# Moving the activation buffers of a two-layer hybrid decoder from byte 192 (and, for one buffer, byte 0) to byte 64, modulo 256, of the weight buffers

## The chip, the core and the metric

One core of one Trainium2 chip runs the whole program. The metric is the time of one execution in microseconds, the median of several runs. The engines are called PE (TensorE, matmuls), PEld (its weight loads, which overlap the matmuls), DVE (VectorE), ACT (ScalarE), POOL (GpSimd) and SP (the queue that issues the DMAs here).

A matmul reads two operands from the core's on-chip memory (SBUF). The *stationary* operand, always 128 columns here, is loaded first, by a weight load of its own; the *moving* operand, 128, 256 or 512 columns, is then streamed past it. While one matmul streams, the load for the next one already runs.

## The reference

The input is 256 tokens of width 1024 in float32. Two layers follow each other, each with a token mixer and a SwiGLU block, each part behind an RMS norm and with a residual add:

```python
y = rms_norm(h, norm_mix[0]);  h = h + hgrn2_mixer(y, ...)   # 8 heads, projections [q|forget|input|gate]
h = h + swiglu(rms_norm(h, norm_ffn[0]), ffn_w13[0], ffn_w2[0])
y = rms_norm(h, norm_mix[1]);  h = h + moba_mixer(y, ...)    # 8 heads, causal attention with a bias table
h = h + swiglu(rms_norm(h, norm_ffn[1]), ffn_w13[1], ffn_w2[1])
return rms_norm(h, final_norm)

def swiglu(h, w13, w2):                     # hidden width 2816
    g, u = jnp.split(h @ w13, 2, axis=-1)
    return (jax.nn.silu(g) * u) @ w2
```

The gated recurrence (HGRN2) is evaluated in levels, with products of the forget gates; with 256 tokens the attention has one block and is plain causal attention.

## The kernel before

**Weights.** All weight matrices are streamed once, in 206 pieces (`raw`, one DMA each, mostly 128 x 1024). ACT rounds a piece to a high part `whi` (line 412) and DVE subtracts to get the low part `wlo` (line 414). Both go into rings of 6 buffers of 4096 bytes a partition. A 128-column piece of a weight begins at a multiple of 512 bytes in its buffer.

**Activations.** Each activation tile, too, is a high and a low part, of 128 x 256: `xh{k}`, `xl{k}` for the eight slices of a layer's input, in two buffers each that alternate from one use to the next, and `hh{n}`, `hl{n}` for the hidden tiles of the SwiGLU block (n = 0 to 6, hidden tile j uses n = j mod 7). The hidden tiles take over the rings of the recurrence's scaled queries and keys `q1, q2, q4 ... q64` and `k1 ... k64` (`alias`): hh0 and hl0 lie where q1 and k1 lay, again with two buffers that alternate.

**Matmuls.** Every product of a weight and an activation is made of three matmuls (high x high, low x high, high x low), all through line 455. There are two forms. In `mm_w` the weight piece is stationary and the activation moves, 256 columns: the projections by head, the output projections, both gate and up products, and the down product of layer 0. In `mm_x` the activation is stationary and the weight moves, 512 columns: the input and value projections and the down product of layer 1. The products among activations (recurrence scores, attention) are a small rest.

**Order.** A planner in the kernel (`Order`) decides at build time, with costs of its own, in which order each engine's instructions stand. In a SwiGLU block 48 matmuls of a gate and up pair alternate with those of a down product: 24 of 256 columns in layer 0 (to psB), 12 of 512 columns in layer 1 (to psA).

**Layout.** `lay_out` makes the first buffers in a fixed order, one behind the other, so that their places are known: a spacer `lead`, the weight rings (which begin at a multiple of 256 bytes), a spacer `gap`, the activation rings, the query and key rings. Everything else follows behind. q1 and k1 have buffers of 1216 bytes instead of 1024 and spacers of 64 bytes on both sides, which puts the first buffer of each at byte 0 modulo 256 and the second at byte 192.

Of the kernel before, what the change touches and what calls it, by code (L numbers as in the profile page):

```python
# [8 lines left out]
FT = mybir.dt.float32  # L9
# [6 lines left out]
P = 128  # L16
S = 256
# [285 lines left out]
def hybrid_trunk(ctx: ExitStack, tc: tile.TileContext, wts, xT, par, gfin, tab, onehot, masks, out):  # L303
# [4 lines left out]
    sb = ctx.enter_context(tc.tile_pool(name="sb", bufs=1))  # L308
# [3 lines left out]
    rings = {}  # L312

    def ring(tag, shape, bufs, dt=FT):
        if tag not in rings:
            rings[tag] = Ring(lambda: sb.tile(shape, dt, name=tag, tag=tag, bufs=bufs), bufs)
        return rings[tag]
# [4 lines left out]
    def alias(tag, other, shape, dt=FT):  # L322

        o = rings[other]
        wide = [P, S + 48] if other in ("q1", "k1") else shape
        rings[tag] = Ring(lambda: sb.tile(wide, dt, name=tag, tag=other, bufs=o.bufs)[:, :shape[1]], o.bufs)
        rings[tag].past = o.past

    def lay_out():


        sb.tile([P, 96], FT, name="lead")
        for t in ("whi", "wlo"):
            ring(t, [P, SUB], NSUB, FR).make()
        sb.tile([P, 48], FT, name="gap")
        for k in range(KT):
            for part in "hl":
                ring(f"x{part}{k}", [P, S], 2, FR).make()
        for part in "qk":

            sb.tile([P, 16], FT, name=f"gap{part}1")
            rings[f"{part}1"] = Ring(lambda part=part: sb.tile([P, S + 48], FT, name=f"{part}1", tag=f"{part}1",
                                                              bufs=2)[:, :S], 2)
            rings[f"{part}1"].make()
            sb.tile([P, 16], FT, name=f"gap{part}2")
        for m in (2, 4, 8, 16, 32, 64):
            for part in "qk":
                ring(f"{part}{m}", [P, S], 2).make()

# [30 lines left out]
    plan = weight_plan()  # L380
    RAW, NSUB = 6, 6
    lay_out()
    segs, c0 = [], 0
    for n in FIRST + (SUB,) * ((NCOLS - sum(FIRST)) // SUB):
# [529 lines left out]
    for n, m in enumerate((1, 2, 4, 8, 16, 32, 64)):  # L914
        alias(f"hh{n}", f"q{m}", [P, S], FR)
        alias(f"hl{n}", f"k{m}", [P, S], FR)
    alias("lg", "mov", [P, 2, 192])
    alias("pt", "sq", [P, 512])
    x1 = {k: X("x", k) for k in range(KT)}
# [371 lines left out]
```

## Time and profile before

| | |
|---|---|
| median of 3 runs | 629.64 us (629.41 to 631.18) |
| span of the profiled execution, first to last instruction | 629.2 us |
| PE busy | 617.4 us, 98% of the span, 4848 matmuls |
| DVE, ACT busy | 441.0 us (70%), 364.2 us (58%) |
| read from device memory | 109.78 MB, 176 GB/s over the span |
| mean granted PE clock | 0.995 |

The median stands 0.4 us above the profiled span. In the profile a matmul's duration goes from its start to the end of its results, so the durations of neighbours overlap; how fast matmuls follow each other is read from the chain of work that ended last, which gives a start, a length and a count for each stretch: length by count is the distance from one matmul to the next. In a row like `psB<-xh,whi` the names are output, moving operand, stationary operand; in a form with the weight moving the weight stands first. The stages of the execution are: input projection to 28 us, recurrence to 137 us, its output projection to 167 us, SwiGLU of layer 0 to 328 us, value projection and norm to 357 us, attention with its projections to 444 us, output projection to 466 us, SwiGLU of layer 1 to 622 us, final norm.

### The profile page before, as it was taken

The page shows a single profiled execution, that of the slowest core. Times are in us where ns is not written, and L with a number is a line of the kernel's source. Part 1 is how long each engine was busy: PE and PEld are TensorE (multiplying, and loading weights), DVE is VectorE, ACT ScalarE, POOL GpSimd, SP SyncE. Part 2 cuts the span into 40 slices and gives each one's busy share as a digit, 9 for nine tenths or more (in the row PEclk, how much of TensorE's full clock was granted, in tenths as well). Part 3 has the DMA queues.
Part 4 walks back from the last instruction along what each step waited for, and adds up shares of the span by engine and source line. Part 5 has one row for each costly group of instructions (what it writes and reads, how often), then busy time and mean ns, then how long its engine had stood idle before and what let it go on. Part 6 is the DMA issues. An engine that isn't in the chain of part 4 may idle for free.

```text
span 629.2 us, 12441 instructions
## 1 busy us (share of the span) xinstructions
PE 617.4 (98%) x4848; PEld 594.2 (94%) x4848; DVE 441.0 (70%) x800; ACT 364.2 (58%) x715; POOL 39.2 (6%) x74
## 2 busy tenths in 40 slices
PE   7999999999999999999999999999999999999995
PEld 5899999999999999999998899999899999999994
DVE  5898878877786666666659678866686666666653
ACT  6798888875564444444446566564674444444443
POOL 0132112200400000000000000000100000000003
PEclk9999999999999999999999999999999999999998
DMA  8964443534896666666653564445545665555501
GB/s 273 324 217 136 154 128 123 155 115 134 209 282 200 194 199 198 190 189 198 201 189 116 209 223 160 143 154 182 180 160 197 201 199 197 177 188 176 168 1 67
DMA packets 32135, 111.83 MB, mean 178 GB/s; under 512 B 3835, under 2 KB 4508, under 8 KB 32076
## 3 DMA queue, kind: packets, MB, share of 16 engines
q1 hardware_dynamic: 31052, 108.71, 53.4%
q0 software_dynamic: 448, 1.25, 1.0%
q10 hardware_dynamic: 576, 1.08, 0.6%
q8 instruction: 38, 0.62, 0.4%
q14 instruction: 21, 0.17, 0.1%
HBM read 109.78 MB, written 1.25 MB: 176 GB/s over the span
## 4 chain that ended last, share of the span: by engine, by line
PE 78%; issue 16%; DVE 3%; DMA 1%; ACT 1%; POOL 1%; SPq 0%; ACTq 0%; DVEq 0%; POOLq 0%
PE psB L455 44%; PE psA L455 33%; DMA raw<-in_w_dram 1%; DVE wlo L414 1%; POOL ny L591 1%; DVE xl L541 0%; DVE yt L607 0%; ACT whi L412 0%; DVE hT L609 0%; DVE sqacc L559 0%; PE psB L1146 0%; SPq L401 0%; SPq L522 0%; PE psA L596 0%; DVE raw L1177 0%
## 5 line engine op out<-in xcount | busy, mean ns | idle before, releaser
L414 DVE TENSOR_TENSOR wlo<-raw,whi 128x1024 fp32r<-128x1024 f32 (+1 forms) x206 | 247.8, 1213 | 107.8 <-ACT whi L412 107.4
L412 ACT ACTIVATE whi<-raw 128x1024 fp32r<-128x1024 f32 (+1 forms) x205 | 213.0, 1050 | 145.7 <-issue 66.7
L455 PE MATMUL psB<-xh,whi 128*128 128x256 f32 x608 | 172.6, 287 | 0.0
L455 PE MATMUL psB<-xh,wlo 128*128 128x256 f32 x608 | 167.6, 279 | 0.0
L455 PE MATMUL psB<-xl,whi 128*128 128x256 f32 x608 | 163.3, 279 | 0.0
L455 PE MATMUL psA<-xh,whi 128*128 128x256 f32 x544 | 150.3, 280 | 0.0
L455 PE MATMUL psA<-xh,wlo 128*128 128x256 f32 x544 | 148.8, 277 | 0.0
L455 PE MATMUL psA<-xl,whi 128*128 128x256 f32 x544 | 144.0, 277 | 0.0
L455 PEld LDWEIGHTS psB<-xh,wlo 128*128 128x128 f32 x608 | 114.6, 188 | 0.7
L455 PEld LDWEIGHTS psB<-xh,whi 128*128 128x128 f32 x608 | 114.4, 188 | 0.8
L455 PEld LDWEIGHTS psB<-xl,whi 128*128 128x128 f32 x608 | 112.2, 189 | 0.0
L455 PEld LDWEIGHTS psA<-xh,whi 128*128 128x128 f32 x544 | 102.4, 188 | 0.6 <-issue 0.5
L455 PEld LDWEIGHTS psA<-xh,wlo 128*128 128x128 f32 x544 | 102.2, 188 | 0.0
L455 PEld LDWEIGHTS psA<-xl,whi 128*128 128x128 f32 x544 | 99.2, 188 | 0.0
L455 PE MATMUL psB<-hl,whi 128*128 128x256 f32 x176 | 48.7, 277 | 0.0
L455 PE MATMUL psB<-hh,whi 128*128 128x256 f32 x176 | 48.7, 277 | 0.0
L455 PE MATMUL psB<-hh,wlo 128*128 128x256 f32 x176 | 48.7, 276 | 0.0
L957 ACT ACTIVATE u<-sgq 128x256 f32<-128x256 f32 x44 | 18.0, 410 | 38.9 <-DVE sgq L955 38.7
L455 PE MATMUL psA<-wlo,hh 128*128 128x512 f32 x88 | 34.6, 393 | 0.0
L455 PE MATMUL psA<-whi,hl 128*128 128x512 f32 x88 | 34.5, 392 | 0.0
L455 PE MATMUL psA<-whi,hh 128*128 128x512 f32 x88 | 34.5, 392 | 0.0
L455 PEld LDWEIGHTS psB<-hl,whi 128*128 128x128 f32 x176 | 33.1, 188 | 0.0
(178 smaller groups left out, 793.8 us busy)
## 6 DMA issues: line engine op xcount, KB each, us to landing
raw<-in_w_dram SPq DMA_DIRECT2D x202, 512.0 KB, 4.2
raw<-in_w_dram SPq DMA_DIRECT2D x4, 256.0 KB, 3.3
bt<-scr POOLq DMA_DIRECT2D x8, 128.0 KB, 9.1
hT<-in_x_dram SPq DMA_DIRECT2D x4, 128.0 KB, 5.1
hT<-in_x_dram SPq DMA_DIRECT2D x2, 256.0 KB, 8.1
bt<-in_final_dram ACTq DMA_DIRECT2D x1, 512.0 KB, 5.4
out_dram<-raw ACTq DMA_DIRECT2D x2, 256.0 KB, 2.2
out_dram<-raw SPq DMA_DIRECT2D x2, 256.0 KB, 2.0
```

The source lines that it names most:

```text
L412: od.op("A", ca(n), lambda h=h, r=r, o=o, n=n: A.activation(h[:, :n], r[:, o:o + n], AF.Copy), reads=[r], alloc=[h], due=due)
L414: od.op("V", cv(n), lambda h=h, lo=lo, r=r, o=o, n=n: V.tensor_tensor(lo[:, :n], r[:, o:o + n], h[:, :n].bitcast(FT), op=OP.subtract), rea ...
L455: T.matmul(o, a, b, start=start, stop=stop, skip_group_check=True)
L591: od.op("G", 500, lambda: G.tensor_tensor(y.tile, v.tile, mhalf, op=OP.pow), reads=[v], alloc=[y], due=due)
L957: od.op("A", ca(S), lambda: A.activation(sg.tile, gs.tile, AF.Sigmoid), reads=[gs], alloc=[sg], due=due)
```

## The change

Only the places of buffers change. The spacer behind the weights shrinks from 192 to 64 bytes, the extra width and the spacers of q1 and k1 go.

```diff
     def alias(tag, other, shape, dt=FT):
         o = rings[other]
-        wide = [P, S + 48] if other in ("q1", "k1") else shape
-        rings[tag] = Ring(lambda: sb.tile(wide, dt, name=tag, tag=other, bufs=o.bufs)[:, :shape[1]], o.bufs)
+        rings[tag] = Ring(lambda: sb.tile(shape, dt, name=tag, tag=other, bufs=o.bufs), o.bufs)
         rings[tag].past = o.past
 
     def lay_out():
         sb.tile([P, 96], FT, name="lead")
         for t in ("whi", "wlo"):
             ring(t, [P, SUB], NSUB, FR).make()
-        sb.tile([P, 48], FT, name="gap")
+        sb.tile([P, 16], FT, name="gap")
         for k in range(KT):
             for part in "hl":
                 ring(f"x{part}{k}", [P, S], 2, FR).make()
-        for part in "qk":
-
-            sb.tile([P, 16], FT, name=f"gap{part}1")
-            rings[f"{part}1"] = Ring(lambda part=part: sb.tile([P, S + 48], FT, name=f"{part}1", tag=f"{part}1",
-                                                              bufs=2)[:, :S], 2)
-            rings[f"{part}1"].make()
-            sb.tile([P, 16], FT, name=f"gap{part}2")
-        for m in (2, 4, 8, 16, 32, 64):
+        for m in (1, 2, 4, 8, 16, 32, 64):
             for part in "qk":
                 ring(f"{part}{m}", [P, S], 2).make()
```

First byte of the buffers in a partition, modulo 256:

| | before | after |
|---|---|---|
| whi, wlo | 0 | 0 |
| xh, xl; hh1 to hh6, hl1 to hl6 (q2 to q64, k2 to k64) | 192 | 64 |
| hh0, hl0 (q1, k1): first, second buffer | 0, 192 | 64, 64 |
| hT, u, xsf, ff, mov | 32 | 160 |
| raw | 96 | 224 |
| sgq | 160 | 32 |

On every engine the same instructions stand in the same order in both programs, with the same waits; only the numbers at the end of some buffer names differ.

## Prediction

> **What bounds the kernel now.** I read the busy times first, then the chain that ended last, then the busy times by stage.
>
> ```profile
> PE 617.4 (98%) x4848; PEld 594.2 (94%) x4848; DVE 441.0 (70%) x800; ACT 364.2 (58%) x715; POOL 39.2 (6%) x74
> PE 78%; issue 16%; DVE 3%; DMA 1%; ACT 1%; POOL 1%; SPq 0%; ACTq 0%; DVEq 0%; POOLq 0%
> ...
> 167.00:328.00 161.00, 161.00 (x1420) 161.00 (x1419) 104.59 (x147) 76.84 (x104) 0.79 (x2) 1.00 0.67 206
> ...
> 526.00:608.00 82.00, 82.00 (x592) 77.23 (x591) 51.64 (x68) 37.52 (x49) 0.00 (x0) 1.00 0.49 159
> ```
>
> The stage rows give the stretch, its length, then the busy time of PE, PEld, DVE, ACT and POOL, the granted clock and the DMA share. PE never idles in either SwiGLU stage, the clock is full, and DVE and ACT have a third of the time to spare. So the end is set by how closely matmuls follow each other, and a nanosecond on each shows in the sum. The chain shows that this distance isn't one number. Start, length, work, count, first in layer 0, then in layer 1:
>
> ```profile
> 184.14 5.46 PE psA L455 x48
> 189.59 2.72 PE psB L455 x24
> 192.31 5.44 PE psA L455 x48
> ...
> 290.23 5.44 PE psA L455 x48
> 295.67 2.86 PE psB L455 x24
> ...
> 516.01 2.75 PE psA L455 x12
> 518.75 5.47 PE psB L455 x48
> 524.22 2.73 PE psA L455 x12
> 526.96 5.66 PE psB L455 x48
> 532.61 2.77 PE psA L455 x12
> 535.38 5.66 PE psB L455 x48
> ```
>
> Call *relation* the byte of the moving operand minus that of the stationary one, modulo 256. The x48 rows have relation 192 (weights at 0, activations at 192), and so have the x24 rows but the one at 295.67: there the hidden tile is j = 14, whose hh0 and hl0 lie at byte 0, relation 0. (j = 0 has these buffers too; j = 7 and 21 have the second ones, at 192.) From these rows:
>
> - relation 192, 256 columns: 5.44 us / 48 = 113.3 ns, or 5.66 / 48 = 117.9 ns. Two paces, each steady for long.
> - relation 0, 256 columns: 2.86 / 24 = 119.2 ns, against 2.72 / 24 = 113.3.
> - 512 columns, where activation and weight change roles: at byte 192 the relation is 0 - 192 = 64: 2.75 / 12 = 229.2 ns, or 2.77 / 12 = 230.8. The group at 524.22 is tile j = 7 with its buffers at byte 0, relation 0: 2.73 / 12 = 227.5. Twice the shortest distance of 256 columns would be 226.7.
>
> So places do matter, by up to 6 ns a matmul, and the row at 524.22 is followed by a change of pace (5.47 to 5.66) that lasts to 608 us: the pace has a memory, set by what came before, and the place alone doesn't fix it.
>
> How much is lost in all at relation 192? In the groups by line, the mean duration of a matmul is 276 ns in the stretch from 200 to 290 us (113.3 apart) and 281 ns from 527 to 608 us (117.9 apart). Below are one row of each stretch, and then the rows of the whole execution:
>
> ```profile
> L455 PE MATMUL psA<-xh,wlo 128*128 128x256 f32 x176 | 48.6, 276 | 0.0
> ...
> L455 PE MATMUL psB<-xh,wlo 128*128 128x256 f32 x160 | 45.0, 281 | 0.0
> ```
>
> ```profile
> L455 PE MATMUL psB<-xh,whi 128*128 128x256 f32 x608 | 172.6, 287 | 0.0
> L455 PE MATMUL psB<-xh,wlo 128*128 128x256 f32 x608 | 167.6, 279 | 0.0
> L455 PE MATMUL psB<-xl,whi 128*128 128x256 f32 x608 | 163.3, 279 | 0.0
> L455 PE MATMUL psA<-xh,wlo 128*128 128x256 f32 x544 | 148.8, 277 | 0.0
> L455 PE MATMUL psA<-xl,whi 128*128 128x256 f32 x544 | 144.0, 277 | 0.0
> L455 PE MATMUL psB<-hl,whi 128*128 128x256 f32 x176 | 48.7, 277 | 0.0
> L455 PE MATMUL psB<-hh,wlo 128*128 128x256 f32 x176 | 48.7, 276 | 0.0
> ```
>
> Over the floor of 276 ns stand 3 ns on 3 x 608 (I give the first row, which also holds restarts after the recurrence's small matmuls, the value of its two sisters), 1 ns on 3 x 544 and 0.6 ns on 3 x 176: 5.5 + 1.6 + 0.3 = 7.4 us of duration. Five ns of duration are 4.6 ns of distance, so 6.8 us of the span, 1.7 ns for each of 3984 matmuls of 256 columns.
>
> **The change part by part.** It adds and removes no instruction, wait or transfer, and moves none in its queue. What it changes is the relation: 256 columns go from 192 (and 0) to 64, 512 columns from 64 (and 0) to 192. Products among activations keep relation 0.
>
> *256 columns.* No matmul of 256 columns has relation 64 before. Bounds from the nearest rows: 113.3 ns below (nothing lost, a gain of 6.8 us), 119.2 above (5.9 x 3984 = 23.5 us lost in place of 6.8, so 16.7 us worse). Nearest is the only row at relation 64, the 512-column one: 229.2 - 226.7 = 2.5 ns lost per matmul. It has no clean stretch: both paces of the 256-column rows around it leave it at 2.75 to 2.77, and its durations spread:
>
> ```profile
> L455 PE MATMUL psA<-whi,hh x88: 388/392/398, 465.7 to 621.3; 128*128 128x512 f32 x88
> L455 PE MATMUL psA<-wlo,hh x88: 389/394/395, 465.9 to 621.5; 128*128 128x512 f32 x88
> ```
>
> (minimum, median, maximum; the median is 4 to 5 ns above the minimum.) Each matmul of either width covers one weight load, so I take 2.5 ns per matmul for 256 columns too: 2.5 x 3984 = 10.0 us, against 6.8 now, +3.2 us.
>
> *512 columns.* There are 456 (88 x 3 in layer 1, 32 x 6 in the two projections). They lose 2.5 to 4.1 ns now, say 3 x 456 = 1.4 us. At relation 192 I give them the mean of the 256-column rows there, 1.7 x 456 = 0.8 us: -0.6 us, between -1.4 and +0.7.
>
> *The hidden tile at byte 0.* Four of its 44 uses go (two with 24 matmuls at 119.2, contained in the sum above), and with them what may start the slow pace at 526.96: ten groups of 48 at 4.6 ns, 2.2 us, also inside the 6.8.
>
> *DVE and ACT.* Their operands move as well. The two instructions that write the hidden tiles wrote them at byte 0 and at 192 already:
>
> ```profile
> L963 ACT ACTIVATE hh<-u x44: 396/408/420, 174.5 to 610.2; 128x256 fp32r<-128x256 f32 x44
> L964 DVE TENSOR_TENSOR hl<-u,hh x44: 417/422/427, 176.3 to 610.7; 128x256 fp32r<-128x256 f32 x44
> ```
>
> A spread of 10 ns (DVE) and 24 ns (ACT) on work that has a third of each stage free costs nothing while PE is the bound. If that cover failed, 24 ns on 44 instructions would be 1.1 us; below, the same as a gain.
>
> *DMA.* raw moves from byte 96 to 224, neither at a boundary of 256. Only the first 28 us wait for it:
>
> ```profile
> 0.00:28.00 28.00, 24.53 (x99) 19.41 (x100) 19.84 (x40) 18.69 (x30) 2.29 (x9) 0.94 0.87 298
> ```
>
> No row shows another start byte. One per cent of the 28 us either way is 0.3 us; I take 0, the row for byte 96.
>
> Sum: 3.2 - 0.6 = +2.6 us on a span of 629.2, so 631.8; with the 0.4 us between span and median, 632.2, given as **632**.
>
> **A rule weighed against the trace.** The rows say that reading the moving operand and loading the next weights disturb each other: 119.2 or 113.3 ns for the same 24 instructions, by place alone. The Trainium skill, "TensorE: Matmul & The Clock Gate", section "Step-by-step: what each phase is for", says that PE has two independent read ports and that loading the next weights doesn't take read bandwidth from the running matmul. By that rule the terms for 256 and 512 columns are both 0 and the time stays. The trace disagrees at relation 0 by 5.9 ns a matmul; at 64 no 256-column row can show it.
>
> **The rivals.**
>
> - *Clean at 64 (faster).* Loads and matmuls no longer meet. For it: pace 113.3 exists, and relation 0 costs 5.9 ns with 256 columns but next to nothing with 512 (2.73 for 12), so the widths needn't share an answer and the 2.5 ns at 64 may not carry over. Against it: the only rows at 64 lose time throughout. Gain 6.8 us, 512 columns -0.6: 629.6 - 7.4 = 622.2 us. It decides from a loss below 1.3 ns a matmul.
> - *Always the slow pace (much slower).* At 64 the matmuls settle at 117.9 everywhere, as after 526 us. For it: that pace lasts once entered. Against it: nothing shows that it is entered more easily. 4.6 x 3984 = 18.3 us instead of 6.8, less 0.6: 629.6 + 10.9 = 640.5 us.
> - *No difference.* What sets the pace is its history, not the place: one relation, 192, shows both 113.3 and 117.9. Then a similar mixture comes out, 629.6 us, within 2 us. The skill's rule above gives the same time, for another reason.
>
> **How the numbers follow.** Chances: the forecast (a loss near 2.5 ns everywhere, 630.5 to 635 us) 0.35, clean 0.27, slow pace 0.20, no difference 0.18. About 0.3% (1.9 us) is what a measurement can tell from no change. Slower: 0.30 of the forecast's 0.35 and the slow pace, 0.50. Faster: clean and 0.03 of the no-difference case, 0.30. Same: the rest, 0.20. The range goes from 622 (clean) to 642 (slow pace everywhere); outside lie relation 0's pace on all (646) and a clean 512-column part on top of the clean case (621). The likeliest case's own range is 630.5 to 635.
>
> **What would show it.** In the changed profile the x48 rows of both SwiGLU stages should stand near 5.56 us (115.8 ns), neither 5.44 nor 5.66, mean durations of 256 columns near 279 everywhere; the x24 rows should all be alike, without a 2.86; the x12 rows should fall towards 2.74. Rows of 5.44 throughout mean the clean rival; 5.66 or more throughout, the slow pace; both mixed in long stretches, no difference. The counts and the order of DVE and ACT work must stay as they are; a stage where PE stops being busy would make the whole argument wrong.

## The result, and the profile after

The changed kernel takes 634.79 us (median of 4 runs, 634.32 to 635.15) against 629.66 us before (629.41 to 631.18): ratio 1.0072, 95% interval 1.0058 to 1.0086. It is slower by 5.1 us, twice the 2.6 of the sum, inside the range and just inside the upper end of the likeliest case's own range (630.5 to 635).

The profiled execution has a span of 632.8 us; its own time is 634.61, so 1.8 us lie outside the span. In all later executions of the kernel before this part is 1.7 to 1.9 us as well. So its profile, with a span of 629.2 us, is that of an execution of some 631 us, near the upper end of 629.41 to 631.18, and the 0.4 us between median and span isn't time spent outside the span. The granted clock shows what probably set it apart: 0.72 as a mean from 14 to 20 us in that profile, 1.00 in the one after. From the start to 28 us the two programs do the same work, but the same matmul stands at 28.1 us before and at 26.9 after. From there to the end the distance grew by 5.0 us, and this is what has to be explained.

First the busy times, then the groups by line that answer to those of before (count, busy time, mean duration of one):

```profile
PE 621.8 (98%) x4848; PEld 596.6 (94%) x4848; DVE 441.0 (70%) x800; ACT 364.5 (58%) x715; POOL 40.9 (6%) x74
...
L447 PE MATMUL psB<-xh,wlo 128*128 128x256 f32 x608 | 167.8, 279 | 0.0
L447 PE MATMUL psB<-xl,whi 128*128 128x256 f32 x608 | 163.5, 280 | 0.0
```

Counts, and the busy time of DVE and ACT, are those of before. The matmul groups of 256 columns have moved by 1 ns at most, some not at all. As a mean over the execution that looks like a small uniform price. The chain of work that ended last shows that it isn't one. First the start of the SwiGLU block of layer 0, then layer 1 (start, length, work, count):

```profile
167.29 0.22 PE psB L588 x2
167.51 13.38 PE psA L447 x118
180.89 2.72 PE psB L447 x24
183.61 5.44 PE psA L447 x48
...
504.66 5.65 PE psB L447 x48
510.31 2.80 PE psA L447 x12
513.11 5.65 PE psB L447 x48
```

Layer 0 runs at 5.44 / 48 = 113.3 ns, the *fast* pace, from its first row (13.38 / 118 = 113.4) to its end. Layer 1 runs at 5.65 / 48 = 117.7 ns, the *slow* pace, throughout. No row stands near 5.56. The 512-column rows at relation 192 take 2.80 / 12 = 233.3 ns, more than the 2.75 to 2.77 of before, and the shortest durations are longer by 4 to 5 ns (the medians by 0 to 2):

```profile
L447 PE MATMUL psA<-whi,hh x88: 392/394/398, 467.0 to 624.9; 128*128 128x512 f32 x88
L447 PE MATMUL psA<-wlo,hh x88: 394/394/402, 467.2 to 625.1; 128*128 128x512 f32 x88
```

PE remains busy in both blocks, at full granted clock (stretch, its length, busy time of PE, PEld, DVE, ACT and POOL, clock, DMA share, GB/s), so waits of other engines play no part:

```profile
167.30:328.00 160.70, 160.70 (x1420) 160.70 (x1419) 104.78 (x147) 77.28 (x105) 0.12 (x1) 1.00 0.65 205
...
526.00:608.00 82.00, 82.00 (x581) 76.45 (x580) 51.51 (x70) 36.96 (x49) 0.00 (x0) 1.00 0.53 167
```

The order of the matmuls is the same in both programs, so the starts of the same matmul can be subtracted. Worked out so from the two traces, with the mean distance of consecutive 256-column matmuls (512-column ones in the value projection):

| stage (by its time before) | length before, us | after, us | distance before, ns | after, ns |
|---|---|---|---|---|
| recurrence, 32 to 137 | 104.6 | 105.1 | 115.6 | 116.7 |
| its output projection, to 168 | 30.6 | 30.9 | 116.5 | 117.7 |
| SwiGLU, layer 0, to 328 | 160.3 | 160.0 | 113.6 | 113.3 |
| value projection and norm, to 357 | 29.0 | 29.4 | 228.8 (512) | 233.0 (512) |
| attention, to 420 | 63.0 | 64.3 | 114.2 | 117.3 |
| to 444 | 24.2 | 23.9 | 117.8 | 117.8 |
| output projection, to 466 | 21.7 | 22.3 | 113.5 | 117.8 |
| SwiGLU, layer 1, first part, to 526 | 60.2 | 61.9 | 113.9 | 117.8 |
| SwiGLU, layer 1, rest, to 622 | 95.6 | 96.2 | 117.8 | 117.8 |

So nothing was lost where most of the work is, in layer 0, and 4.3 of the 5.0 us came from attention, the output projection behind it and the SwiGLU block of layer 1, from 256 columns that were fast before and are slow now, and from the 512 columns.

### The profile page after: what moved, and what is told of

It reads as the page before. It is cut to its first block, busy times and chain, and to the rows that moved or that the text cites. A ratio compares the mean times of both kernels' runs of the same rounds, so it can differ in the third digit from the quotient of the medians.

```text
span 632.8 us, 12441 instructions
## 1 busy us (share of the span) xinstructions
PE 621.8 (98%) x4848; PEld 596.6 (94%) x4848; DVE 441.0 (70%) x800; ACT 364.5 (58%) x715; POOL 40.9 (6%) x74
## 4 chain that ended last, share of the span: by engine, by line
PE 76%; issue 17%; DVE 3%; POOL 1%; DMA 1%; ACT 1%; SPq 0%; DVEq 0%; ACTq 0%; POOLq 0%
PE psB L447 43%; PE psA L447 33%; DVE wlo L406 1%; POOL ny L583 1%; DMA raw<-in_w_dram 1%; DVE xl L533 1%; DVE sqacc L551 1%; DVE yt L599 0%; ACT whi L404 0%; DVE hT L601 0%; PE psB L1138 0%; SPq L393 0%; SPq L514 0%; PE psA L588 0%; DVE sqacc L572 0%
## 5 line engine op out<-in xcount | busy, mean ns | idle before, releaser
L447 PEld LDWEIGHTS psB<-xh,wlo 128*128 128x128 f32 x608 | 114.2, 188 | 0.8
L447 PEld LDWEIGHTS psB<-hh,whi 128*128 128x128 f32 x176 | 33.0, 188 | 0.0
```

Source lines behind the costliest of these rows:

```text
L447: T.matmul(o, a, b, start=start, stop=stop, skip_group_check=True)
```

## The experiments

The first question was which operand's place matters, and whether the pace is set by the place or carried over from the work before it. All kernels below change only spacers and buffer widths unless they say otherwise, and their diffs are against the changed kernel. Ratios are to the kernel before, run on the same chip.

**All activations at 192, without a buffer at byte 0.** This is the kernel before without its one exception.

```diff
-        sb.tile([P, 16], FT, name="gap")
+        sb.tile([P, 48], FT, name="gap")
```

> Layout of before, but q1 and k1 (hh0, hl0) too lie at byte 192 in both buffers; everything behind stays where before has it. Theory 'place' (each relation has its own price): only the two x24 groups at 2.86 us become 2.72, about 629.4 us. Theory 'inheritance' (256 columns at relation 192 or 64 can run at 113.3 or at 117.9 ns, and a stretch takes over the pace that the 512-column group ahead of it leaves; relation 0 at tile j = 7 started the slow one): no group at relation 0 is left to start it, so all x48 rows of the SwiGLU block of layer 1 stay at 5.47 us, 2 us less there, about 627.4 us.

Measured: 627.43 us (626.97 to 628.67), ratio 0.9960 (0.9944 to 0.9976). It is faster than both. The chain in layer 0 and layer 1:

```profile
182.94 5.44 PE psA L447 x48
...
500.79 5.47 PE psB L447 x48
506.26 2.75 PE psA L447 x12
509.00 5.47 PE psB L447 x48
```

Layer 1 now stays at 5.47 / 48 = 114.0 ns. Its second part up to 608 us of before, which ran at 117.8, shrinks from 82.0 to 80.0 us. So the slow pace there was started by the hidden tile at relation 0 and lasted to the end of the block: at relation 192 a single odd tile cost 2 us behind it. (Not every such tile does: in layer 0 of before, the x48 rows behind both tiles at relation 0 stand at 5.46.) Without it, the 512-column matmuls at relation 64 in between didn't disturb the fast pace; with it, they didn't end the slow one.

**Inputs at 192, hidden tiles at 64, and the reverse.**

```diff
-        sb.tile([P, 16], FT, name="gap")
+        sb.tile([P, 48], FT, name="gap")        # reverse: 16
             for part in "hl":
                 ring(f"x{part}{k}", [P, S], 2, FR).make()
+        sb.tile([P, 32], FT, name="gaph")       # in both
```

(The first has another spacer of 128 bytes behind the key rings.)

> Inputs xh, xl at byte 192 as before, hidden tiles (q, k rings) at 64 as after. In layer 1's SwiGLU the 512-column groups have relation 192, the 256-column groups 192 as before. Place: x12 rows 2.80 us as after, x48 rows as before (5.47), about 630.5 us. Inheritance: x12 rows 2.80, and x48 rows 5.65 throughout, though their operands lie as in before; attention and its projections keep the pace of before; about 632 us.

> Inputs at byte 64 as after, hidden tiles at 192. In layer 1's SwiGLU the 512-column groups have relation 64, the 256-column groups 64. Place: x12 rows 2.75 us, x48 rows 5.65 as after, about 633.7 us. Inheritance: x12 rows 2.75 and x48 rows 5.47 throughout though their operands lie as in after; attention at the slow pace as after (the value projection's 512 columns have relation 192); about 630.5 us.

Measured: with inputs at 192 and hidden tiles at 64, 634.01 us (632.21 to 634.25), ratio 1.006 (1.004 to 1.008). Here is the chain, in layer 0 and in layer 1:

```profile
179.99 2.83 PE psB L449 x24
182.81 5.45 PE psA L449 x48
...
503.64 5.46 PE psB L449 x48
509.10 2.79 PE psA L449 x12
511.89 5.66 PE psB L449 x48
517.55 2.80 PE psA L449 x12
520.35 5.46 PE psB L449 x48
```

In layer 0 the input groups (192) are fast and the hidden groups (64) between them slow, 2.83 / 24 = 117.9. So a fast stretch at 192 doesn't carry over into 64 here: all 17 x24 rows of layer 0 are slow right behind a fast group. In layer 1 the hidden tile is the stationary operand, so the x12 rows have relation 192, and the x48 rows around them alternate between fast and slow. I had expected this alternation from neither theory.

The reverse took 640.08 us (639.81 to 640.64), ratio 1.0156 (1.0139 to 1.0174):

```profile
184.22 5.66 PE psA L448 x48
189.87 2.83 PE psB L448 x24
...
507.87 2.77 PE psA L448 x12
510.64 5.65 PE psB L448 x48
```

Everything of 256 columns in the SwiGLU blocks is slow, in layer 0 too, where the changed kernel with the same input places was fast, and the x24 rows are slow although they have relation 192. The slow layer 0 as such can't be put down to the hidden tiles: the spacer of this kernel also moves all buffers behind the key rings, and a test below shows layer 0 slow from that move alone. But the x48 groups at 192 above were fast behind slow groups at 64, and the x24 groups at 192 here were not. A pace that is simply carried on, or simply regained at a place, does not give both these kernels.

**The distance by relation, matmuls alone.** A kernel that computes nothing of the reference runs groups of 48 matmuls of 256 columns and of 12 or 24 of 512 at chosen relations, each behind 512-column ones of relation 0, 64, 128 or 192, with no other engine at work.

> Matmuls alone, the computation left out (zeros as output): 32 blocks, each 12 matmuls of 512 columns at relation 0, 64, 128 or 192 and then 48 of 256 columns at one of 8 relations in steps of 32. Place: the 256-column distance depends on its own relation alone, the same after all four. Inheritance: relations 64 and 192 show 113.3 ns after 512 columns at relation 64 and 117.9 after relation 0 or 192. Both: 256 columns at relation 0 near 120 ns, 512 columns at 0 near 226.7, at 64 near 229, at 192 near 233; 128 is open and may be clean in both forms.

Measured (one execution of 287.8 us). In a name like `n192after64x` stand the relation of the 256-column group and that of the 512-column group ahead of it:

```profile
17.67 5.75 PE n0after0x L336 x48
...
102.10 5.65 PE n64after64x L336 x48
...
136.01 5.47 PE n192after64x L336 x48
...
271.35 5.45 PE n192after192x L336 x48
```

| relation | 0 | 32 | 64 | 96 | 128 | 160 | 192 | 224 |
|---|---|---|---|---|---|---|---|---|
| 256 columns, ns | 119.8 | 116.7 | 117.8 | 120.0 | 118.6 to 120.0 | 117.3 to 118.7 | 113.6 to 113.9 or 117.8 | 118.3 |
| 512 columns, once settled, ns | 226.7 | | 229 | | 231.9 | | 233.4 | |

At 64 the 256-column groups took 117.8 behind all four kinds of 512-column groups; at 192 they took 113.6 to 113.9 behind 64 and 192, 117.8 behind 0 and 128. For 512 columns the cost rises with the relation, and 192 is the dearest of the four. With matmuls alone the difference between relation 0 and 192 is still 5.75 against 5.45 for 48. The Trainium skill, "TensorE: Matmul & The Clock Gate", section "Step-by-step: what each phase is for", has two independent read ports, with no read bandwidth taken from the running matmul by the next load. These rows disagree in so far as the place of the operands would then cost nothing, and here no other engine is at work; what it is that the two reads share isn't shown. Nor is it shown that the *relation* counts and not the place of the activation by itself: in all kernels here the weights begin at multiples of 256 bytes, and only the activations were moved.

**Does the fast pace at 64 depend on how it is entered?** The changed kernel was fast at 64 in layer 0 and the matmuls alone, so far, never were. The first of two tests puts the query and key buffers, and with them the tile of j = 0, at byte 0, then 64; the second leaves the operands of the big matmuls where they are and moves only the buffers behind them (`raw`, `hT`, `u` and others) back to the bytes of before. The first diff is shortened.

```diff
+            # first test: spacers around q1 and k1, as in the kernel before
+            sb.tile([P, 48 if part == "q" else 32], FT, name=f"gap{part}1")
+            ... sb.tile([P, S + 16], FT, name=f"{part}1", tag=f"{part}1", bufs=2)[:, :S]
```
```diff
+        # second test: behind the key rings
+        sb.tile([P, 32], FT, name="tail")
```

> After, with the other part of the change undone: q1 and k1 (hh0, hl0) lie at byte 0 in the first and at 64 in the second buffer, everything else as in after. Place: two x24 groups of layer 0 go from 2.72 to 2.86, +0.3 us, about 635. Regain (both relations can hold the fast pace of 113.3 ns, but after a disturbance only 192 finds back to it; 64 keeps the slow one): from tile j = 0 on, at about 184 us, all 256-column rows of layer 0's SwiGLU run at 117.9 ns, x48 rows 5.65 in place of 5.44, some 1250 matmuls by 4.5 ns, +5.6 us, about 640.5 us.

> After, with 128 bytes of spacer behind the key rings, so that raw, hT and all later buffers lie at the byte that before has; weights, activations, queries and keys as in after. If only the relation of a matmul's two operands counts: the time of after, 634.8 us, within 1 us. If the other buffers' places carry a part of the 5 us: back towards 630.

Measured: the first, 641.47 us (640.68 to 641.98), ratio 1.0173 (1.0136 to 1.0210):

```profile
168.79 13.38 PE psA L454 x118
182.17 2.88 PE psB L454 x24
185.04 5.66 PE psA L454 x48
```

Layer 0 is entered fast (13.38), and from the tile of relation 0 on (2.88) it is slow and stays slow: 165.9 us instead of 160.0. Every other buffer has the byte, modulo 256, of the changed kernel, so this is what came before, not the place. The second, 641.23 us (640.48 to 642.32), ratio 1.0173 (1.0140 to 1.0206):

```profile
167.29 0.22 PE psB L589 x2
167.51 13.90 PE psA L448 x118
181.41 2.83 PE psB L448 x24
184.23 5.65 PE psA L448 x48
```

Here the same two small matmuls of plain float32 stand at the same time as in the changed kernel, and behind them the same 118 matmuls, operands at the same relation, run at 13.90 / 118 = 117.8 instead of 113.4. Layer 0 takes 166.3 us instead of 160.0. Nothing that PE reads in the SwiGLU matmuls moved. The moved buffers don't slow PE as such either, for in the output projection ahead of the block it is the other way round. First the changed kernel, then the one with the moved buffers:

```profile
142.25 9.19 PE psB L447 x78
...
142.99 8.85 PE psB L448 x78
```

These are 256 columns at 64 as well: 9.19 / 78 = 117.8 against 8.85 / 78 = 113.5. At 64 each of the two kernels shows both paces, in different places. So in the changed kernel the fast pace of layer 0 is an accident of what lies ahead, and is worth 6.3 us: with all its activations at 64, the kernel can just as well take 641 us. What exactly ahead of the block decides it isn't shown.

**All at 128.**

```diff
-        sb.tile([P, 16], FT, name="gap")
+        sb.tile([P, 32], FT, name="gap")
```

(and a 64-byte spacer behind the key rings.)

> All activations, queries and keys at byte 128, the rest as before. From the sweep (256 columns at relation 128: 118.5 to 120.0 ns, never 113.3; 512 columns 232): place and regain both give about 119 ns on 3984 matmuls in place of a mean of 115, +16 us, and +1 us for 512 columns: about 645 us. If 128 can hold the fast pace where nothing disturbs it, as in layer 0's SwiGLU: about 638 us.

Measured: 646.23 us (644.92 to 647.41), ratio 1.0250 (1.0216 to 1.0285). The x48 rows stand at 5.69 to 5.70 and the x24 rows at 2.84 to 2.85, 118.7 ns in both layers, as the matmuls alone had it at 128 behind two of the four 512-column groups (5.69 and 5.70; 5.76 behind the other two). There is no stretch at 113.3 anywhere.

**What frees the pace at 64.** With matmuls alone again (one execution of 244.7 us, nothing computed): 256-column groups at 64 and 192 behind a slow group, behind relation 0, and behind 2 to 5 plain float32 matmuls (two records each in the trace); and finer steps of the relation.

> Matmuls alone, the computation left out (zeros as output). The same 256 columns at relation 64 after five histories: a stretch at 192 that runs fast, 512 columns, relation 0, and 2 to 5 plain float32 matmuls. Regain: 113.3 ns straight after the fast stretch and kept for all 96, 117.8 after 512 columns and after relation 0; relation 192 finds 113.3 after every one but relation 0 and 512 columns at 0. Place: 117.8 after all. The 14 relations in finer steps are open: only multiples of 64 have been fast so far.

```profile
18.05 5.65 PE n192afterwide64x L336 x48
23.71 11.31 PE n64afterfast192x L336 x96
...
71.63 0.44 PE plainx L344 x4
72.07 5.45 PE n64afterplain2yx L336 x48
...
84.09 5.66 PE n64afterplain3yx L336 x48
```

At 64 one group was fast: the one behind two plain matmuls (5.45; behind three, four and five 5.66). The row before the x96 group, which was to give it a fast start, was itself slow (5.65), so this kernel does not say what 64 does directly behind a fast stretch. With plain matmuls between, the groups at 64 behind two (fast) and three (slow) had a fast group at 192 ahead, those behind four and five a slow one. Behind a group at relation 0, the group at 64 was slow (5.66) and the one at 192 fast (5.46). Of fourteen finer relations, 16 to 240, none was fast; they ran from 5.52 (112) to 5.84 (200).

The two plain matmuls were then put into the slow kernel with the moved buffers, ahead of hidden tile 6 of layer 0, two in one kernel and three in another:

```diff
             b = main_bank(gu)
+            for _ in range(2 if (layer, j) == (0, 6) else 0):        # or 3
+                mm(b[:, :P], ident, ident, start=True, stop=True)
```

> The layout of e5_tail to the byte (activations at 64, all later buffers where before has them), plus two plain float32 matmuls of 128 columns (the identity by itself, into a bank that is overwritten right behind) ahead of hidden tile 6 of layer 0's SwiGLU, near 185 us. History: the pace behind them is set anew; if it is the fast one, x48 rows go from 5.65 to 5.44 us from there on and the time falls by up to 1150 x 4.5 ns = 5 us in spite of the added work, to about 636 us; if the slow one, 641.5. Place: 5.65 us as before, 641.5 us.

> As e8_tail_plain2 with three plain matmuls in place of two. History: it need not be the same pace as behind two; in the test of matmuls alone two left the fast pace and three the slow one, so about 641.5 us here if the count decides. Place: 641.5 us in both.

Measured: 640.85 us (640.74 to 641.70), ratio 1.0183 (1.0166 to 1.0200), and 641.40 us (641.32 to 641.90), ratio 1.0190 (1.0173 to 1.0207). The chain with two, behind the place:

```profile
198.62 2.83 PE psB L448 x24
```

Neither got layer 0 out of the slow pace (166.7 and 166.9 us): at this place neither two nor three plain matmuls end it.

**192 with the other buffers moved.** The same test of robustness as above, for 192: all activations at 192, the buffers behind them at the bytes of the changed kernel.

```diff
-        sb.tile([P, 16], FT, name="gap")
+        sb.tile([P, 48], FT, name="gap")
+        sb.tile([P, 32], FT, name="tail")       # behind the key rings
```

> All activations, queries and keys at byte 192 as in e1_all192, but the later buffers (raw, hT and behind) at the bytes that after has. At byte 64 this place of the later buffers is worth 6.4 us (after 634.8, e5_tail 641.2). If 192 finds back to the fast pace after most disturbances: within 2 us of e1_all192, 627.4, with 5.44 and 5.47 us in the x48 rows. If the good time of 192 is a lucky history too: up to 6 us slower, 633.

Measured: 628.45 us (10 runs, 628.04 to 629.00), ratio 0.9980 (0.9970 to 0.9989). Both SwiGLU blocks stay fast: 160.0 us in layer 0, and x48 rows of 5.47 in layer 1. It takes 1.0 us more than the other layout at 192. In the profiles it loses in the recurrence (0.3), in attention (0.5) and in the output projection to 466 us, where 256 columns run at 117.6 instead of 113.5 (0.6), and gets 0.7 back in the stretches to 168 and from 420 to 444 us. At 64 the same kind of shift cost 6.4 us. The four layouts together separate the two causes: with the other buffers where the changed kernel has them, the activations at 64 take 634.8 us and at 192 628.5; with the other buffers where the kernel before has them, 641.2 and 627.4.

**How often each place is entered fast.** Matmuls alone (one execution of 317.9 us, nothing computed): a 256-column group of 24 at 64 or 192, behind one to eight plain float32 matmuls, then 512 columns at 64 or 192, then a 256-column group again; 16 entries of each kind at each relation.

> Matmuls alone, the computation left out (zeros as output): 32 times 1 to 8 plain float32 matmuls, 24 of 256 columns, 12 of 512 columns at relation 64 or 192, 24 of 256 columns again, half with the 256 columns at relation 64, half at 192. Regain as now put (plain matmuls leave either pace at both relations; after 512 columns only 192 is fast): the x24 rows behind plain matmuls are a mixture of 2.72 and 2.83 us at both relations; behind 512 columns all 16 at relation 64 are 2.83, and most of the 16 at 192 are near 2.73 to 2.76. Place: one length for each relation throughout. Pure history (no relation favours a pace): mixtures of about the same share in all four groups.

```profile
168.90 2.80 PE wide64x L328 x12
171.69 2.74 PE n192afterwide64yx L336 x24
...
240.63 2.74 PE n192afterplain1yx L336 x24
243.37 2.79 PE wide192x L328 x12
246.16 2.83 PE n192afterwide192yx L336 x24
...
249.44 2.74 PE n192afterplain2yx L336 x24
...
254.97 2.83 PE n192afterwide192yx L336 x24
...
258.46 2.83 PE n192afterplain3yx L336 x24
261.30 2.80 PE wide192x L328 x12
264.10 2.74 PE n192afterwide192yx L336 x24
```

| group of 24 at relation | behind plain matmuls | behind 512 at 64 | behind 512 at 192 |
|---|---|---|---|
| 64 | 0 of 16 fast | 0 of 8 | 0 of 8 |
| 192 | 7 of 16 | 8 of 8 | 4 of 8 |

All 32 groups at 64 were slow (2.83). None had a fast stretch ahead of it, so this shows that nothing here ended the slow pace at 64, and not what 64 does with a fast one. At 192 the pace follows from the pace before. Behind an odd number of plain matmuls it was the same as ahead of them, behind an even number the other one, in 16 of 16 (the first had a slow group at 64 ahead). 512 columns at relation 192 turned it over, fast to slow and slow to fast, in 8 of 8. 512 columns at relation 64 led into the fast pace in all 8, whatever the pace before; elsewhere they needn't, since the row at 18.05 above is slow behind such a group, and the kernel before stayed slow through ten of them. So 7 of 16 and 4 of 8 are no chances of independent tries: another sequence would give other counts. The turning over by 512 columns at 192 agrees with the alternation of the x48 rows with hidden tiles at 64 and inputs at 192. What the kernels share is that the slow pace ends more easily at 192 than at 64.

## Why the prediction was right, and where it wasn't

*What bounds the kernel* held: PE was busy in every long stage, the distance of matmuls was the whole effect, and the counts of DVE and ACT work stayed.

*256 columns: 2.5 ns per matmul, 10.0 us lost against 6.8, +3.2.* The sum came out and the reason did not. Counted over the 3803 distances below 130 ns between consecutive 256-column matmuls of weight and activation, before lost 5.7 us over 113.3 ns (1.5 ns each) and after 9.6 us (2.5 ns each), so +3.9. But the 2.5 is the mean of two paces: nothing lost in layer 0 (all 1409 distances fast) and some 4.5 ns in most of the rest (2141 of the other 2394 are not fast). The failed step is the transfer of the price from the 512-column rows at relation 64 to 256 columns. At 64 there is no price of 2.5 ns; there are 113.3 and 117.8. With the other buffers moved it is 117.8 in the long stages, and the kernel takes 641.2. That the mean met the forecast is a coincidence of how long the fast stretch happened to be.

*512 columns: −0.6.* Wrong in sign: 233.3 at relation 192 against 229 to 230 at 64, +1.0 us over the layer-1 groups and +0.4 in the value projection. The step that failed here is the same: taking the mean of 256-column rows (1.7 ns) for 512 columns. The widths follow different rules, as the hint at relation 0 (5.9 ns with 256, next to nothing with 512) already said; I had used that hint only for the clean rival. With 256 columns (+3.9) and 512 (+1.4), 5.3 us stand against the 5.0 measured behind 28 us; the other 0.3 isn't accounted for. The sum itself, +2.6, was half of the 5.1 measured.

*Span and median, 0.4 us.* No run shows such a cost: the profile came from an execution above the median, and 1.7 to 1.9 us lie outside the span. Since the sum began at that span and ended at the median, it came out as if it had begun at the median.

*The hidden tile at byte 0.* The reading of the chain was right: it started the slow pace in layer 1. The kernel without it got back 2.0 us there, where 2.2 were reckoned. The changed kernel also removes it but doesn't get this gain, since at 64 it is slow there anyhow.

*DVE and ACT, DMA: 0.* Busy times hardly changed (441.0 us; 364.2 to 364.5). The matmul at 28 us stands between 26.7 and 28.2 us in the whole kernels run here, in no order by the place of `raw`. No experiment isolated them.

*The rivals.* "Always the slow pace" gave 640.5 us; the layout with all activations at 64 and the other buffers moved measured 641.2, the one with all but one buffer each of two tiles at 64 measured 641.5. It was right for layer 1, attention and the output projections, and missed by one condition, that layer 0 is entered fast. "Clean at 64" was right for layer 0 alone. "No difference: history, not place" had half of the mechanism, the memory, but not its other half, that the place decides how readily the fast pace returns. I had written against the slow pace that nothing shows it to be entered more easily at 64. In the runs it is held more easily there: 641.2 and 634.8 us at 64 against 627.4 and 628.5 at 192.

*What stays open.* What fixes the pace inside PE or the memory isn't shown: places, widths and what went ahead decide it, but no rule found here gives every row. Relation and place of the activation alone weren't told apart, since the weights never moved. With inputs at 64 and hidden tiles at 192 the x24 groups at 192 were slow behind slow groups at 64; with the places exchanged the x48 groups at 192 were fast behind slow groups at 64. What brought layer 0 of the changed kernel into the fast pace, out of a slow stretch at 64, isn't known.

## What to carry to other kernels

Where PE is always busy, divide chain rows by their counts, stage by stage, before believing a mean: two paces hid here behind one mean of 279 ns. In a kernel of this form (weights at multiples of 256 bytes, 128 stationary columns), place the moving operand of 256 columns 192 bytes modulo 256 behind the stationary one, with no exception, and let wider moving operands sit at relation 64 or 0: all activations at 192 took 627.4 us, 0.4% less than before and 1.2% less than the changed kernel. And test a layout by shifting the buffers that have nothing to do with it; a gain that goes away under that (6.4 us at 64, 1.0 us at 192) was luck.

## What the runs showed of the hardware that I had not expected

- Of the tested relations only 64 and 192 let 256 columns run at 113.3 ns; 0 gives 119.8, 128 118.6 to 120.0 alone and 118.7 in the kernel. For 512 columns the order is another one: 226.7 at 0 once settled, 229 at 64, 231.9 at 128, 233.4 at 192.
- At 64 and 192 the distance has two values, 113.3 and 117.8, each of which can last: 160 us or more in layer 0 at either value with identical relations.
- With matmuls alone, 512 columns at 192 turned the pace at 192 over in 8 of 8, and an even number of plain float32 matmuls between two stretches at 192 did so too, an odd number did not (16 of 16). In that kernel no group at 64 was fast (0 of 32); one of the 12 groups at 64 in the two kernels before that was fast.
